# Where an overflow pass stands among 32 streamed experts, and how often their counts are asked

## The chip, the cores and the metric

One core of a Trainium2 chip. The metric is the device time of one execution in microseconds (us); the lower the better. The profiled execution is one such execution with the hardware profiler's records.

## The reference

One block of a streaming encoder on 256 tokens of width 1024: projections, three branches (sparse latent attention, convolution, memory attention), a mix and a layer norm give `h`; then a mixture of experts on `h`, a residual and a last layer norm. What the change touches is the mixture, cut to its core:

```
logits = h @ w_router + b_router                 # 256 x 32
top_v, top_e = top_k(logits, 4)
gate = softmax(top_v)
for e in range(32):                              # tokens that chose e
    g, u = split(h[tokens] @ w1[e] + b1[e], 2)   # w1[e]: 1024 x 2048
    g, u = min(g, 7), clip(u, -7, 7)
    a = (u + 1) * (g * sigmoid(1.702 * g))
    y[tokens] += gate * (a @ w2[e] + b2[e])      # w2[e]: 1024 x 1024
out = layer_norm(alpha * h + y)
```

## The kernel before, in words

Until about 300 us the kernel computes everything up to the router; it counts the tokens of each expert (`cnt`), each token's place within its expert (`pos`) and its gate (`Gt`). Then the experts follow one after another, e0 to e31, and at the end the layer norm.

*Weights.* Each expert has 12 tiles of 1 MB, eight of `w1` and four of `w2`. SP sends them in order (`send`, L107 and L109) into a ring of 20 slots; a send waits until the slot's earlier tile has been used, and what stands behind it on SP waits too. All weights are used once, so that 384 tiles pass through the ring.

*Tokens.* An expert works in blocks of 32 tokens: block 0 always, block 1 only with more than 32 tokens, block 2 with more than 64 (conditionals on the count, which `load` brings into registers of PE, ScalarE and VectorE, L1263). What one expert has beyond 96 goes to passes over a list after e31 (`passes`, `more`), each up to 96 tokens of one expert, which load that expert's 12 tiles again. `more` is nested ten deep; each depth asks the list whether there is another pass (L1296), and an untaken one is left by a branch over all that is nested in it. With this input four experts have three blocks (e5, e8, e10, e25), eight have two (e0, e7, e12, e13, e15, e16, e17, e27), twenty have one; e25 alone has tokens for a pass (44 of them). It can be seen in the trace from the bias products of a block (L1085 into PG, PU, PY), which stand at its start.

*One expert* (`products`, L1175). First products of all blocks into PG, PU and PY (`first`, L1085 for the bias, L1088 for the weights); the scatter of the expert before into the accumulators PO (`scatter`, L1141); the activation on VectorE and ScalarE (`act`, L1092 to L1098); the rows of the next expert, taken out of `h` by a product with a 0/1 matrix (`onehot` L1039, `gather` L1045), which are then transposed (`turn_x`, L1052); the activations transposed (`turn_a`, L1102); second products, in two halves (`second`, L1110 for the bias, L1118), and between them the places of the next expert's tokens (`places`, L1123 and L1124, on PX) and what VectorE makes of them for the scatter (`slots`, L1128, L1129). `split_y` (L1134, L1135) reads the result. A third block shares buffers: its activation waits for that of block 0 (L1190 to L1194), its scatter is done at once (`third_out`, L1161). Conditionals stand after each pair of first products (L1075), around the activation (L1185), the turns (L1190, L1192), the second products (L1075), `split_y` (L1202) and the third blocks (L1233). The engines run the same program; each has its own register and branches by itself.

*e0* has its places and slots made before its products (L1340 to L1344). Its residual (`residual`, L1173) follows its first products.

*The end.* After e31 its scatter, then `more(0, ...)`, then four closing products (L1358), the rows of `r` (L1364) and the layer norm (L1373 to L1387).

The order of the instructions on each engine is that of the code, as a scheduler has slightly shifted it; no table sets it.

Of the kernel before, what the change touches and what calls it, by code (L numbers as in the profile page):

```python
# [75 lines left out]
def tile_block(ctx: ExitStack, tc: tile.TileContext, x, memt, wf, wsm, bp, wdw, rows, w1, b1, w2, b2, out):  # L76
# [995 lines left out]
    def past(n, f, b=1):  # L1072

        if b < 3:
            with tc.If(n > 32 * b):  # L1075
                f(b)
                past(n, f, b + 1)
# [43 lines left out]
    def places(x):  # L1121

        PE.matmul(PX[:, 0:T], lhsT=x.idb.to_broadcast([NE, 128]), rhs=posT, start=True, stop=True)  # L1123
        PE.matmul(PX[:, T:2 * T], lhsT=x.idf.to_broadcast([NE, 128]), rhs=GT, start=True, stop=True)  # L1124

    def slots(x, b, sc, gs):

        V.tensor_scalar(sc, PX[:, 0:T], x.sx[b], None, op0=OP.is_equal)  # L1128
        V.scalar_tensor_tensor(g, sc.bitcast(F32), 1.0, PX[:, T:2 * T], op0=OP.mult,  # L1129
                               op1=OP.mult, accum_out=gs)  # L1130
# [30 lines left out]
    def third_out(x, p):  # L1161

        scatter(s2s[p], y2)
        places(x)
        slots(x, 2, s2s[p], g2[p])
        split_y(PG, g2[p], y2)
# [8 lines left out]
    def products(x, p, n, before=None, rows=None, turned=None, beside=None):  # L1175


        banks = (PG, PU, PY)
        xs = [xcol(xT, 0), xcol(xT, 1), xcol(x2, 0)]
        for k in range(0, KD, 2):  # L1180
            first(x, xs[0], PG, (k, k + 1))
            past(n, lambda b: first(x, xs[b], banks[b], (k, k + 1)))
        before and before()
        act(PG[:, 0:256], PG[:, 256:512], ab[:, 0, :])
        with tc.If(n > 32):  # L1185
            act(PU[:, 0:256], PU[:, 256:512], ab[:, 1, :])
        rows and rows()
        turn_a(ab[:, 0, :], PG[:, 0:256], aT[0])
        turned and turned()
        with tc.If(n > 32):  # L1190
            turn_a(ab[:, 1, :], PU[:, 0:256], aT[1])
            with tc.If(n > 64):  # L1192
                act(PY[:, 0:256], PY[:, 256:512], ab[:, 0, :])
                turn_a(ab[:, 0, :], PG[:, 256:512], aT[2])  # L1194
        outs = (PY, PU, PG)
        second(x, aT[0], PY, 0)
        past(n, lambda b: second(x, aT[b], outs[b], 0))
        beside and beside()
        second(x, aT[0], PY, 1)
        past(n, lambda b: second(x, aT[b], outs[b], 1))  # L1200
        split_y(PY, gc[p], ys)
        with tc.If(n > 32):  # L1202
            split_y(PU, g2[p], y2)
# [4 lines left out]

    def expert(e, prev, n, nxt):
        p = e % 2  # L1210
        x, last = Work(e), nxt is None
        y = None if last else Work(e + 1)

        def before():
            if not e:
                return residual()
            scatter(scs[1 - p], ys)
            with tc.If(prev > 32):
                scatter(s2s[1 - p], y2)

        def beside():
            places(y)
            slots(y, 0, scs[1 - p], gc[1 - p])
            with tc.If(nxt > 32):
                slots(y, 1, s2s[1 - p], g2[1 - p])

        if last:
            products(x, p, n, before)
        else:
            onehot(y, 0, dd)  # L1230
            products(x, p, n, before, lambda: gather(dd), lambda: turn_x(xT), beside)
            send_to(e + 1)
        with tc.If((n if last else n | nxt) > 64):  # L1233
            with tc.If(n > 64):
                third_out(x, p)
            if not last:
                with tc.If(nxt > 64):
                    third_in(y)
# [26 lines left out]

    three_e = [ET.PE, ET.Activation, ET.DVE]

    def count(e):
        return load(cnt[0:1, e:e + 1], three_e, 256) if e < NE else None
# [25 lines left out]
    def more(j, w):  # L1295
        with tc.If(load(ki[0:1, j:j + 1], three_e + [ET.SP], 64) > 0):  # L1296
# [7 lines left out]
            onehot(x, 0, dd)  # L1304
            gather(dd)
            turn_x(xT)
            n = load(un, three_e, 256)
            places(x)
            for b in range(2):
                slots(x, b, (scs, s2s)[b][0], (gc, g2)[b][0])  # L1310
            with tc.If(n > 64):
                third_in(x)
            products(x, 0, n)
            scatter(scs[0], ys)
            with tc.If(n > 32):
                with tc.If(n > 64):
                    third_out(x, 0)
                scatter(s2s[0], y2)
# [12 lines left out]
    tokens_in()  # L1331
# [6 lines left out]
    counts = [None, count(0), None]  # L1338
    x = Work(0)
    places(x)  # L1340
    slots(x, 0, scs[0], gc[0])
    with tc.If(counts[1] > 32):
        slots(x, 1, s2s[0], g2[0])
    with tc.If(counts[1] > 64):  # L1344
        third_in(x)
    for e in range(NE):
        if e == 1:
            passes()
        counts[2] = count(e + 1)
        expert(e, *counts)  # L1350
        counts = counts[1:] + [None]
    scatter(scs[(NE - 1) % 2], ys)
    with tc.If(counts[0] > 32):
        scatter(s2s[(NE - 1) % 2], y2)
    more(0, {b: big("w") for b in [(1, k) for k in range(KD)] + [(2, c) for c in (0, 2, 1, 3)]})
# [103 lines left out]
```

## Time and profile before

| | us |
|---|---|
| median of 3 runs | 1339.78 |
| lowest and highest run | 1336.41, 1343.5 |
| profiled execution | 1340.14 |
| its span, first to last instruction | 1338.4 |
| PE busy (share of the span) | 1096.7 (82%) |
| VectorE busy | 469.5 (35%) |
| ScalarE busy | 291.5 (22%) |
| DMA queue of the kernel, share of 16 engines | 86.1% |

The shares are means over two stages: until 300 us PE works on the branches while little is loaded, afterwards 32 experts are streamed. The windows below cut the second stage. A row of a timeline gives start, duration, engine, line, operation, tiles, the number of instructions drawn together, and in brackets for how long the engine was idle before it and what released it.

### The profile page before, as it was taken

What the parts mean: (1) busy time and instruction counts of PE and PEld (TensorE: products, weight loads), DVE (VectorE), ACT (ScalarE), POOL (GpSimd) and SP (SyncE); (2) the same over time, 40 slices, a digit from 0 to 9 for tenths busy, and PEclk for the clock granted to TensorE, in tenths of its full rate; (3) what the DMA queues carried; (4) which work ended last, traced back from release to release, by engine and by line L of the source; (5) the groups of instructions that cost most, each with busy time, mean ns of one, the idle gap of its engine ahead of it and who ended that gap; (6) DMA issues with size and microseconds to landing.
All of it is one profiled execution on the core that took longest, in us unless ns stands there. A gap on an engine that the chain in (4) does not pass through costs nothing. (4 is left out here: it accounts for less than half of the span.)

```text
span 1338.4 us, 22356 instructions
## 1 busy us (share of the span) xinstructions
PE 1096.7 (82%) x8154; PEld 518.2 (39%) x8154; DVE 469.5 (35%) x1098; ACT 291.5 (22%) x561; POOL 96.3 (7%) x105
## 2 busy tenths in 40 slices
PE   9899889988777888988888888887876698877673
PEld 7788679952222222223222222232221123322121
DVE  6897998762222122221212212222111122221123
ACT  6457875631011010011101101111010001010000
POOL 1406660010000000000000000000000000000001
PEclk9899999999998989989989999999998898999887
DMA  7654258687999999969799999999999999999971
GB/s 272 219 188 132 90 190 318 222 301 315 406 423 419 422 423 422 404 239 404 277 371 417 366 407 423 392 384 420 422 423 421 421 424 422 420 421 421 421 325 66
DMA packets 88075, 464.29 MB, mean 347 GB/s; under 512 B 8209, under 2 KB 8337, under 8 KB 54001
## 3 DMA queue, kind: packets, MB, share of 16 engines
q1 hardware_dynamic: 87888, 461.78, 86.1%
q8 instruction: 120, 1.97, 0.5%
q14 instruction: 67, 0.54, 0.1%
HBM read 460.70 MB, written 1.05 MB: 345 GB/s over the span
## 5 line engine op out<-in xcount | busy, mean ns | idle before, releaser
L1088 PE MATMUL PG<-w,RES 128*32 128x512 f32 x2112 | 293.5, 670 | 40.1 <-PEq L1075 21.7
L1088 PEld LDWEIGHTS PG<-w,RES 128*32 128x32 f32 x2112 | 71.3, 117 | 230.3 <-issue 172.7
L1092 DVE TENSOR_SCALAR RES<-PG 128x256 f32<-128x256 f32 x33 | 14.0, 425 | 402.6 <-PE PG L1088 402.6
L1118 PE MATMUL PY<-w,aa 128*32 128x512 f32 x1056 | 139.7, 622 | 2.0 <-DMA w<-in_w_dram 1.4
L1093 ACT ACTIVATE RES<-RES 128x256 f32<-128x256 f32 x50 | 20.9, 417 | 503.2 <-DVE RES L1092 503.0
L264 PE MATMUL mm<-hh,whi 128*128 128x256 f32 x352 | 102.4, 291 | 6.9 <-DVE gt L799 3.0
L265 PE MATMUL mm<-hl,whi 128*128 128x256 f32 x352 | 99.1, 282 | 4.1 <-DVE hl L364 4.1
L1088 PE MATMUL PU<-w,RES 128*32 128x512 f32 x832 | 100.5, 599 | 0.0
L266 PE MATMUL mm<-hh,wlo 128*128 128x256 f32 x352 | 98.7, 280 | 0.2 <-DVE wlo L218 0.2
L1045 PE MATMUL PX<-h,dd 128*64 128x512 f32 x296 | 77.9, 648 | 24.9 <-DVE dd L1039 13.7
L218 DVE TENSOR_TENSOR wlo<-raw,whi 128x1024 fp32r<-128x1024 f32 (+1 forms) x74 | 92.0, 1252 | 10.1 <-ACT whi L210 6.6
L210 ACT ACTIVATE whi<-raw 128x1024 fp32r<-128x1024 f32 (+1 forms) x74 | 76.0, 1030 | 18.0 <-DMA raw<-in_wf_dram 17.8
L138 POOL TENSOR_TENSOR l20r<-l20a,mhalf 128x1 f32<-128x1 f32 x1 | 0.6, 550 | 1029.5 <-DVE l20a L136 1029.5
L264 PEld LDWEIGHTS mm<-hh,whi 128*128 128x128 f32 x352 | 66.8, 190 | 11.3 <-DVE gt L799 3.2
L1085 PE MATMUL PG<-BB,sel 96*32 96x512 bf16 x128 | 16.1, 460 | 65.5 <-DVEq L1233 50.8
L265 PEld LDWEIGHTS mm<-hl,whi 128*128 128x128 f32 x352 | 66.6, 189 | 4.9 <-DVE hl L364 4.6
L664 POOL TENSOR_TENSOR cv<-cv,ct 128x256 f32<-128x256 f32 x70 | 63.7, 910 | 57.2 <-ACT ct L663 52.6
L266 PEld LDWEIGHTS mm<-hh,wlo 128*128 128x128 f32 x352 | 66.6, 189 | 0.4 <-DVE wlo L218 0.4
L1134 ACT ACTIVATE yy<-PY,gc 128x512 fp32r<-128x512 f32 x33 | 22.7, 687 | 194.2 <-PE PY L1118 187.7
L1128 DVE TENSOR_SCALAR sc<-PX,sx 128x256 fp32r<-128x256 f32 x32 | 15.5, 484 | 133.7 <-PE PX L1124 133.7
L1118 PEld LDWEIGHTS PY<-w,aa 128*32 128x32 f32 x1056 | 40.3, 112 | 52.2 <-issue 35.9
L1118 PE MATMUL PU<-w,aa 128*32 128x512 f32 x416 | 54.9, 599 | 0.0
(363 smaller groups left out, 1386.4 us busy)
## 6 DMA issues: line engine op xcount, KB each, us to landing
w<-in_w_dram SPq DMA_DIRECT2D x396, 1024.0 KB, 18.2
raw<-in_wf_dram SPq DMA_DIRECT2D x70, 512.0 KB, 4.0
rb<-in_rows_dram SPq DMA_DIRECT2D x3, 512.0 KB, 6.1
mT<-in_memt_dram SPq DMA_DIRECT2D x4, 256.0 KB, 5.7
raw<-in_wf_dram SPq DMA_DIRECT2D x4, 256.0 KB, 5.1
xt<-in_x_dram SPq DMA_DIRECT2D x2, 512.0 KB, 6.6
rw<-in_rows_dram SPq DMA_DIRECT2D x2, 512.0 KB, 5.1
r<-in_rows_dram SPq DMA_DIRECT2D x2, 512.0 KB, 4.7
```

Source lines behind the costliest of these rows:

```text
L210: S.activation(parts[i][:, c], raw[i][:, c], AF.Copy)
L218: V.tensor_tensor(lo[:, c], raw[i][:, c], parts[i][:, c].bitcast(F32), op=OP.subtract)
L264: PE.matmul(o, lhsT=wh, rhs=xh, start=first, stop=False)
L265: PE.matmul(o, lhsT=wh, rhs=xl, start=False, stop=False)
L266: PE.matmul(o, lhsT=wl, rhs=xh, start=False, stop=last)
L664: G.tensor_tensor(o, o, ct, op=OP.add)
L1045: PE.matmul(PX[q * 64:q * 64 + 64, :], lhsT=dd[:, t, :].bitcast(F32), rhs=h1[:, t, q * 512:q * 512 + 512], start=t == 0, stop=t == 1)
L1085: PE.matmul(y, lhsT=x.sel.to_broadcast([96, 32]), rhs=BB1[:, :, c], start=True, stop=False)
L1088: PE.matmul(y, lhsT=xs(k), rhs=x.w[1, k][:, :, c], start=False, stop=k == KD - 1)
L1093: S.activation(s, g, AF.Sigmoid, scale=1.702)
L1118: PE.matmul(o[r:r + 32, :], lhsT=aT[:, c:c + 32], rhs=x.w[2, k // 2][:, k % 2, q * 512:q * 512 + 512], start=i == 0 and h > 0, stop=i == 3)
L1134: S.activation(y[0], o, AF.Copy, scale=gs)
```

## The change

It does seven things.

1. The passes (`more`) stand between e30 and e31. The scatter of e30 is done before them, the tiles of e31 are sent behind them, and e31's rows, places and slots are made there; e30 and e31 are no longer interleaved.
2. `count` loads a count into three sets of registers: PE's own (`n[0]`), one of ScalarE and VectorE (`n[1]`), one of all three (`n[2]`). A conditional in which only some engines have work uses their register: the first products PE's, the activation that of the other two.
3. The third block's first products go to PX instead of PY, its activation into a buffer of its own (`aT[3]`), directly behind that of block 1.
4. Turns and first halves of the second products of blocks 1 and 2 stand together in one conditional; second halves, `split_y`, `third_out` and the next expert's `third_in` in another (L1206), on `n | m`, the counts of this expert and the next.
5. The gather stands behind all activations in the code, as before, but now shares PX with the third block's products and activation.
6. The loads of the next count stand behind the scatter instead of at the head of the expert.
7. e0: `tokens_in`, the residual, places and slots stand behind its first products, the places on PY.

```diff
-    def products(x, p, n, before=None, rows=None, turned=None, beside=None):
-        banks = (PG, PU, PY)
+    def products(x, p, n, before=None, y=None, counts=None):
+        banks = (PG, PU, PX)
         xs = [xcol(xT, 0), xcol(xT, 1), xcol(x2, 0)]
         for k in range(0, KD, 2):
             first(x, xs[0], PG, (k, k + 1))
-            past(n, lambda b: first(x, xs[b], banks[b], (k, k + 1)))
+            past(n[0], lambda b: first(x, xs[b], banks[b], (k, k + 1)))
         before and before()
+        m = counts() if y else None
         act(PG[:, 0:256], PG[:, 256:512], ab[:, 0, :])
-        with tc.If(n > 32):
+        with tc.If(n[1] > 32):
             act(PU[:, 0:256], PU[:, 256:512], ab[:, 1, :])
-        rows and rows()
+            with tc.If(n[1] > 64):
+                act(PX[:, 0:256], PX[:, 256:512], aT[3])
+        if y:
+            gather(dd)
         turn_a(ab[:, 0, :], PG[:, 0:256], aT[0])
-        turned and turned()
-        with tc.If(n > 32):
+        if y:
+            turn_x(xT)
+        second(x, aT[0], PY, 0)
+        with tc.If(n[2] > 32):
             turn_a(ab[:, 1, :], PU[:, 0:256], aT[1])
-            with tc.If(n > 64):
-                act(PY[:, 0:256], PY[:, 256:512], ab[:, 0, :])
-                turn_a(ab[:, 0, :], PG[:, 256:512], aT[2])
-        outs = (PY, PU, PG)
-        second(x, aT[0], PY, 0)
-        past(n, lambda b: second(x, aT[b], outs[b], 0))
-        beside and beside()
+            second(x, aT[1], PU, 0)
+            with tc.If(n[2] > 64):
+                turn_a(aT[3], PG[:, 256:512], aT[2])
+                second(x, aT[2], PG, 0)
+        if y:
+            slots_in(y, 1 - p, m, PX)
         second(x, aT[0], PY, 1)
-        past(n, lambda b: second(x, aT[b], outs[b], 1))
         split_y(PY, gc[p], ys)
-        with tc.If(n > 32):
-            split_y(PU, g2[p], y2)
+        with tc.If((n[2] | m[2] if y else n[2]) > 32):
+            with tc.If(n[2] > 32):
+                second(x, aT[1], PU, 1)
+                split_y(PU, g2[p], y2)
+                with tc.If(n[2] > 64):
+                    second(x, aT[2], PG, 1)
+                    third_out(x, p)
+            if y:
+                with tc.If(m[2] > 64):
+                    third_in(y)
+    def flush(p, n):
+        scatter(scs[p], ys)
+        with tc.If(n[0] > 32):
+            scatter(s2s[p], y2)
+    def rows_in(y):
+        onehot(y, 0, dd)
+        gather(dd)
+        turn_x(xT)
+    def slots_in(y, p, m, o):
+        places(y, o)
+        slots(y, o, 0, scs[p], gc[p])
+        with tc.If(m[1] > 32):
+            slots(y, o, 1, s2s[p], g2[p])
     def send_to(e):
         while sent[0] < 12 * e + 12:
             send()
...
+    def loads(a):
+        return [load(a, g, 256) for g in ([ET.PE], [ET.Activation, ET.DVE], three_e)]
     three_e = [ET.PE, ET.Activation, ET.DVE]
     def count(e):
-        return load(cnt[0:1, e:e + 1], three_e, 256) if e < NE else None
+        return loads(cnt[0:1, e:e + 1])
...
             x = More(j, w)
-            onehot(x, 0, dd)
-            gather(dd)
-            turn_x(xT)
-            n = load(un, three_e, 256)
-            places(x)
-            for b in range(2):
-                slots(x, b, (scs, s2s)[b][0], (gc, g2)[b][0])
-            with tc.If(n > 64):
+            rows_in(x)
+            n = loads(un)
+            slots_in(x, 0, n, PX)
+            with tc.If(n[2] > 64):
                 third_in(x)
             products(x, 0, n)
-            scatter(scs[0], ys)
-            with tc.If(n > 32):
-                with tc.If(n > 64):
-                    third_out(x, 0)
-                scatter(s2s[0], y2)
+            flush(0, n)
             if j + 1 < NX:
                 more(j + 1, w)
...
     turn_x(xT, True)
-    tokens_in()
...
-    counts = [None, count(0), None]
-    x = Work(0)
-    places(x)
-    slots(x, 0, scs[0], gc[0])
-    with tc.If(counts[1] > 32):
-        slots(x, 1, s2s[0], g2[0])
-    with tc.If(counts[1] > 64):
-        third_in(x)
+    n, m = count(0), None
+    with tc.If(n[2] > 64):
+        third_in(Work(0))
+    prev = None
     for e in range(NE):
         if e == 1:
             passes()
-        counts[2] = count(e + 1)
-        expert(e, *counts)
-        counts = counts[1:] + [None]
-    scatter(scs[(NE - 1) % 2], ys)
-    with tc.If(counts[0] > 32):
-        scatter(s2s[(NE - 1) % 2], y2)
-    more(0, {b: big("w") for b in [(1, k) for k in range(KD)] + [(2, c) for c in (0, 2, 1, 3)]})
+        p = e % 2
+        x, y = Work(e), Work(e + 1) if e < NE - 2 else None
+        def before():
+            nonlocal m
+            if not e:
+                tokens_in()
+                residual()
+                slots_in(x, 0, n, PY)
+            elif e < NE - 1:
+                flush(1 - p, prev)
+            if y:
+                m = count(e + 1)
+        if y:
+            onehot(y, 0, dd)
+        products(x, p, n, before, y, lambda: m)
+        if y:
+            send_to(e + 1)
+            prev, n = n, m
+        elif e == NE - 2:
+            flush(p, n)
+            more(0, {b: big("w") for b in [(1, k) for k in range(KD)] + [(2, c) for c in (0, 2, 1, 3)]})
+            send_to(e + 1)
+            n = count(e + 1)
+            rows_in(Work(e + 1))
+            slots_in(Work(e + 1), 1 - p, n, PX)
+            with tc.If(n[2] > 64):
+                third_in(Work(e + 1))
+    flush(p, n)
```

(`n[2] | m[2]` is a bitwise or.) Two places of the programs as built, in the order in which an engine meets the rows.

SP, from the last tiles of the innermost pass on, before (`w` is a weight tile, `r` the rows of the last layer norm; PE_49 and the like are the counters on which a row waits):

```order
L1302 DMA w<-in_w_dram 128x2x1024 [waits DMAHW6_49,PE_49]
L1075 UNCONDITIONAL_BRANCH
L1202 UNCONDITIONAL_BRANCH
L1315 UNCONDITIONAL_BRANCH
L1296 UNCONDITIONAL_BRANCH [waits SP_sequencer_49,DMAHW0_49,DMAHW1_49,DMAHW2_49,DMAHW3_49,DMAHW4_49,DMAHW5_49,DMAHW6_49,DMAHW7_49] x10
L1364 DMA r_16752<-in_rows_dram 128x1024 [waits DMAHW7_49,PE_49,Activation_49]
```

and now (L1297 and L1303 are the old L1296 and L1302):

```order
L1303 DMA w<-in_w_dram 128x2x1024 [waits DMAHW2_49,PE_49]
L1206 UNCONDITIONAL_BRANCH
L1219 UNCONDITIONAL_BRANCH
L1297 UNCONDITIONAL_BRANCH [waits SP_sequencer_49,DMAHW0_49,DMAHW1_49,DMAHW2_49,DMAHW3_49,DMAHW4_49,DMAHW5_49,DMAHW6_49,DMAHW7_49] x10
L107 DMA w<-in_w_dram 128x2048 [waits DMAHW7_49,DMAHW3_49,PE_49]
L107 DMA w<-in_w_dram 128x2048 [waits DMAHW4_49,DMAHW2_49,DMAHW6_49,DMAHW1_49,PE_49]
L107 DMA w<-in_w_dram 128x2048 [waits DMAHW5_49,DMAHW1_49]
```

The tiles of e31 (L107) were sent ahead of the passes and now stand behind the branch over them; the first two wait on a count of PE that is reached in the last use of a pass's tile in the program, in the tenth nested pass.

PE, from the end of e0's first products (the third block's) to the gather of e1's rows, before:

```order
L1088 MATMUL PY<-w,RES 32x512 [waits Activation_49]
L1088 MATMUL PY<-w,RES 32x512 x7
L1075 UNCONDITIONAL_BRANCH
L1075 UNCONDITIONAL_BRANCH [waits PE_49] x2
L1173 MATMUL PO_3503<-h_3399,ab 128x512 [waits DVE_49,Pool_49]
...
L1185 COMPARE_AND_BRANCH
L1185 UNCONDITIONAL_BRANCH x2
L1045 MATMUL PX<-h_3399,dd 64x512 [waits Activation_49]
```

and now:

```order
L1088 MATMUL PX<-w,RES 32x512 [waits DVE_49,Activation_49]
L1088 MATMUL PX<-w,RES 32x512 x7
L1075 UNCONDITIONAL_BRANCH
L1075 UNCONDITIONAL_BRANCH [waits PE_49] x2
L1023 MATMUL PY<-ident,pos 32x128 x2
L1173 MATMUL PO_3503<-h_3399,ab 128x512 [waits DVE_49,Pool_49]
...
L1123 MATMUL PY<-posT,idb 128x256
L1124 MATMUL PY<-tl,ident 128x256
L1260 TENSOR_LOAD cnt x2
L1045 MATMUL PX<-h_3399,dd 64x512 [waits DVE_49,Activation_49]
```

Between the first products and the gather stand the transposes of `pos` and `Gt` (L1023), the places (L1123, L1124) and the loads of e1's count; the gather waits on VectorE too, and PE has no conditional around the activation any more.

## Rows read from the trace of the kernel before

**Rows 1.** Windows of the second stage; the last columns: granted clock, DMA share, GB/s.

```profile
350.00:550.00 200.00, 162.90 (x1212) 54.74 (x1212) 42.67 (x125) 22.01 (x47) 0.00 (x0) 0.93 1.02 422
550.00:610.00 60.00, 52.52 (x412) 18.84 (x408) 13.03 (x37) 6.59 (x15) 0.00 (x0) 0.94 0.79 309
...
890.00:1290.00 400.00, 308.85 (x2177) 101.41 (x2181) 76.66 (x231) 37.99 (x81) 0.00 (x0) 0.92 1.02 420
```

**Rows 2.** PE timeline of e19 (one block), with its start and the next.

```profile
913.45 0.43 PE L1085 MATMUL PG<-BB,sel 96*32 96x512 bf16 x4 [2.37 <-DVEq L1233]
...
925.34 1.94 PE L1045 MATMUL PX<-h,dd 128*64 128x512 f32 x8 [0.57 <-DVE ab L1098]
...
929.33 0.39 PE L1110 MATMUL PY<-BB,sel 96*32 96x512 bf16 x2 [0.64 <-DVEq L1190]
...
936.55 0.43 PE L1085 MATMUL PG<-BB,sel 96*32 96x512 bf16 x4 [2.37 <-DVEq L1233]
```

**Rows 3.** VectorE timeline of e19: activation from L1092 to L1098, slots L1128.

```profile
923.46 0.42 DVE L1092 TENSOR_SCALAR RES<-PG 128x256 f32<-128x256 f32 x1 [9.42 <-PE PG L1088]
...
924.90 0.49 DVE L1098 SCALAR_TENSOR_TENSOR ab<-ab,RES 128x128 f32<-128x128 f32 x2
...
932.36 0.48 DVE L1128 TENSOR_SCALAR sc<-PX,sx 128x256 fp32r<-128x256 f32 x1 [3.14 <-PE PX L1124]
```

**Rows 4.** PE timeline of e8 (three blocks), start, middle and the next start.

```profile
545.47 0.41 PE L1085 MATMUL PG<-BB,sel 96*32 96x512 bf16 x4
...
574.75 0.44 PE L1102 MATMUL PG<-ident,ab 128*128 128x128 f32 x2 [2.28 <-DVE ab L1098]
...
575.29 2.91 PE L1118 MATMUL PY<-w,aa 128*32 128x512 f32 x16
...
593.50 0.65 PE L1085 MATMUL PG<-BB,sel 96*32 96x512 bf16 x4 [3.01 <-DVEq L1237]
```

**Rows 5.** VectorE timeline of e8: the third block's activation starts.

```profile
572.89 0.41 DVE L1092 TENSOR_SCALAR RES<-PY 128x256 f32<-128x256 f32 x1
```

**Rows 6.** PE timeline of e0: first products, residual, gather, and e1's start.

```profile
300.48 3.19 PE L1088 MATMUL PG<-w,RES 128*32 128x512 f32 x16
...
318.58 3.67 PE L1173 MATMUL PO<-h,ab 128*128 128x512 f32 x8 [0.56 <-DVE ab L1098]
...
322.18 1.94 PE L1045 MATMUL PX<-h,dd 128*64 128x512 f32 x8
...
337.15 0.43 PE L1085 MATMUL PG<-BB,sel 96*32 96x512 bf16 x4 [1.98 <-DVE lg L1251]
```

**Rows 7.** PE timeline: last products of e30, of e31, scatters, closing products.

```profile
1243.68 1.92 PE L1118 MATMUL PY<-w,aa 128*32 128x512 f32 x16
...
1272.27 1.91 PE L1118 MATMUL PY<-w,aa 128*32 128x512 f32 x12 [1.39 <-DMA w<-in_w_dram]
...
1275.82 0.96 PE L1141 MATMUL PO<-yy,sc 64*128 64x512 f32 x6 [0.23 <-DVEq L1202]
...
1318.92 1.20 PE L1141 MATMUL PO<-y__3521,s 64*128 64x512 f32 x8 [0.31 <-PEq L1316]
1324.07 0.27 PE L1358 MATMUL PO<-one,tri 128*128 128x1 bf16 x4 [3.95 <-PEq L1296]
```

**Rows 8.** On PE: the branches at L1233, and the count loads; ns minimum/median/maximum.

```profile
L1233 PEldq COMPARE_BRANCH  x32: 67/215/440, 336.2 to 1274.7; - x32
...
L1263 PEldq TENSOR_LOAD <-cnt x32: 297/306/487, 298.2 to 1224.3; - x32
```

**Rows 9.** PE's branches at L1296, SP's wait for them, the rows of r.

```profile
L1296 PEldq COMPARE_BRANCH  x3: 70/179/3892, 1277.4 to 1323.8; - x3
...
SPq L1364 <- PEq L1296: 21.4, 1, 21.4
...
1323.67 2.03 SPq L1364 DMA_DIRECT2D r<-in_rows_dram  x2
...
DMA to landing us min/median/max: 3.8/4.7/5.6
```

More of the change, by code (lines that the diff above doesn't have):

```diff
@@ L1119, in second, with places, slots @@
                               start=i == 0 and h > 0, stop=i == 3)
[L1121 to L1129, printed above, removed]
+    def places(x, o):
+        PE.matmul(o[:, 0:T], lhsT=x.idb.to_broadcast([NE, 128]), rhs=posT, start=True, stop=True)
+        PE.matmul(o[:, T:2 * T], lhsT=x.idf.to_broadcast([NE, 128]), rhs=GT, start=True, stop=True)
+    def slots(x, o, b, sc, gs):
+        V.tensor_scalar(sc, o[:, 0:T], x.sx[b], None, op0=OP.is_equal)
+        V.scalar_tensor_tensor(g, sc.bitcast(F32), 1.0, o[:, T:2 * T], op0=OP.mult,
                                op1=OP.mult, accum_out=gs)
@@ L1163, in third_out @@
         scatter(s2s[p], y2)
-        places(x)
-        slots(x, 2, s2s[p], g2[p])
+        places(x, PX)
+        slots(x, PX, 2, s2s[p], g2[p])
         split_y(PG, g2[p], y2)
@@ L1207, in send_to @@
             send()
[L1209 to L1233, printed above, removed]
-            with tc.If(n > 64):
[L1235 to L1238, printed above, removed]
     NX = 10
@@ L1303, in more @@
             x = More(j, w)
-            onehot(x, 0, dd)
-            gather(dd)
-            turn_x(xT)
-            n = load(un, three_e, 256)
-            places(x)
-            for b in range(2):
-                slots(x, b, (scs, s2s)[b][0], (gc, g2)[b][0])
-            with tc.If(n > 64):
+            rows_in(x)
+            n = loads(un)
+            slots_in(x, 0, n, PX)
+            with tc.If(n[2] > 64):
                 third_in(x)
             products(x, 0, n)
-            scatter(scs[0], ys)
-            with tc.If(n > 32):
-                with tc.If(n > 64):
-                    third_out(x, 0)
-                scatter(s2s[0], y2)
+            flush(0, n)
             if j + 1 < NX:
@@ L1337, in tile_block @@
     send_to(0)
-    counts = [None, count(0), None]
-    x = Work(0)
-    places(x)
-    slots(x, 0, scs[0], gc[0])
-    with tc.If(counts[1] > 32):
-        slots(x, 1, s2s[0], g2[0])
-    with tc.If(counts[1] > 64):
-        third_in(x)
+    n, m = count(0), None
+    with tc.If(n[2] > 64):
+        third_in(Work(0))
+    prev = None
     for e in range(NE):
```

## The prediction

> **What bounds the kernel now.** I read the windows first, then PE's, VectorE's and SP's timelines, then the waits. From 350 to 550 us and again from 890 to 1290 the DMA share is 1.02 and the stream moves 420 to 422 GB/s; between 550 and 610 it falls to 0.79 and 309 GB/s [rows 1]. An expert is 12 tiles of 1.049 MB, so at 420 GB/s a tile takes 2.5 us and an expert 30. A one-block ("light") expert takes PE 23.1 us from one first bias product to the next (e19, 913.45 to 936.55 [rows 2]), a three-block ("hot") one 48.0 (e8, 545.47 to 593.50 [rows 4]); a two-block ("mid") one lies between. So the ring of 20 slots (50 us of stream) fills in the hot and mid experts, and when it is full SP cannot send: the reader sees it in the window of e8, from 550 on. The DMA's idle time up to 890 is set by **PE**. After 890 the **stream** sets the time: nothing that PE saves there counts. What PE saves from e0 to e17 moves the whole stream earlier (call it G); what comes after the stream's last tile counts in full. These two are the sum.
>
> **G, part by part.** *Light experts.* In e19 PE waits 0.57 at the gather, 0.64 at L1110 and 2.37 at L1085 [rows 2]. L1110 waits for VectorE's walk over the conditional L1190, which is gone: -0.64. The wait at L1085 holds PE's last products (to 934.17), split_y, two conditionals (L1202, L1233) and a register load; one conditional and the load leave: -0.4 (estimate). Against it, the gather now also waits, through PX, for both engines' walk over the new conditional behind the activation: +0.44 taken (an estimate), between 0 (it waits for the activation today, 0.57) and 1.0 (its 1.94 us no longer cover what ends later). Hence about -0.77 with the branch behind `second` that is gone too (0.17); six such experts before e18 give -4.6, and two ahead of a hot one, -0.5 each, -5.6 in all.
> *Hot experts* (e5, e8, e10). In e8 the third block's activation starts at 572.89 [rows 5], because it waits for block 0's buffer, and PE stands 2.28 us at 574.75; the next 16 products take 2.91 us [rows 4] where 16 take 1.92 elsewhere [rows 7]. The activation now goes to a buffer of its own directly behind the second, some 5 us sooner, under the scatter of e7. Then the gather, two transposes and block 0's products follow: these start near 572.7 instead of 575.3. Two new stalls appear, since blocks 1 and 2 are now turned right before their products: each waits about 0.8 for its copies. With -2.5 from the start, -2.2 from products that no longer run slowly, +1.6 from the stalls, a last step unchanged (3.01 before L1085 either way), I take -3.0, bounds -1 and -5: three times, **-9.1**.
> *Loads.* Two more register loads per expert on PE, 0.31 each [rows 8], stand where PE waits for the activation anyway: 0, or 0.6 if that wait should go.
> *Mid experts.* The second block is turned late there too (+0.9), the wait at L1110 (0.6) and part of the end leave (-0.3 to -0.4): 0 each, +0.2 in all.
> *e0.* Its products start earlier: PX's places no longer stand before them, 297.3 for 300.48, so they end near 314.8 instead of 318.0 (the residual's start less its wait [rows 6]). But then come, one behind the other: four transposes (0.9, as two of L1102 [rows 4]) and VectorE's two copies (0.8, as two of L1092 [rows 3]), residual 3.67 [rows 6], places (0.8), slots for two blocks on VectorE (2.0: L1128 at 0.48 [rows 3] and its partner, twice), two register loads (0.6 [rows 8]), and only then two activations of 1.93 each (L1092's start to L1098's end [rows 3]). Before, both ran under the residual, and the gather began at 322.18 [rows 6]. Now 314.8 + 12.6 = 327.4, **+5.2**; the 12 tiles of e0 come free that much later, and the sends that wait for them. PE has idled some 7 us there, and I add 1.4 for slower products behind that (the 16 that took 2.91 or 3.19 instead of 1.92 followed such gaps [rows 4, 6]). Bounds: +0.5, if slots and loads hide, and +8.
> *Clock.* The granted clock is 0.92 to 0.94 in these windows [rows 1]; slow stretches like e8's follow gaps of PE, of which some shrink: 0 to -5, taken -1.7.
> So G = 5.6 + 9.1 - 0.2 - 6.6 + 1.7 = **9.6**, with ends of 1 and 18.
>
> **The end.** Today: e30's last products end at 1245.60, e31's at 1274.18, 1.91 behind its last tile, its scatter at 1276.78, and the pass follows; its scatter ends at 1320.12 [rows 7]. PE then walks over nine nested passes: one branch of 3.892 us; SP has waited 21.4 us for that before it sends the rows of `r` at 1323.67 [rows 9], and L1358 runs at 1324.07 [rows 7]. With the pass ahead of e31, all of this moves up by e31's 28.58 us: pass end 1291.5, branch and signal to 1295.1. **e31's twelve tiles stand behind it.** The order of SP shows their sends behind the branch over the nested passes, and the first two wait on PE's counter as `r`'s send does today: the slots are those of the pass's tiles, whose last use in the program stands in the last nested pass. So nothing of e31 is loaded while the pass computes. From 1295.1 I count 1.9 until the stream runs (half of the 3.8 that the quicker of `r`'s two loads took to land [rows 9]; ends 1 and 3.8), 12 x 2.5 = 30.0, then 1.9 to the last product and 2.6 to the end of the scatter as today: 1331.5. The preparation of e31 (gather, places) lies under the load, and so do its first products. From L1358 to the span's end today are 14.3 us, of which VectorE waits 0.7 for `r`, which now comes earlier: 13.6, with 0.4 to reach it. 1345.5 against 1338.4: **+7.1**, ends +5.5 and +9.5. The pass itself is costed at no change: its tiles take the place in the stream that e31's had, and they land before its products ask for them.
>
> [...] PE's branch over the nested passes takes 3.892 us, that over L1233's 30 rows 0.215 in the median and 0.44 at most [rows 8]. The new L1206 jumps over 36 rows on PE; I cost it as L1233's. [...]
>
> **Sum.** 1340.1 + 7.1 - 9.6 = 1337.6 against the profiled run (1340.14, 0.4 above the median of the three runs, which themselves lie 7 us apart); against the median **1337.2**. Change by over 0.5%, about what a measurement of this kernel can tell from none, begins at 1333.1 and 1346.5.
>
> **Rivals.**
> 1. *PE gains more* (0.17): the hot experts gain 5 each and no stretch behind a shorter gap is slow: G = 16 to 18, about 1329.5. For it: e8's slow products stand right behind its 2.28 us wait [rows 4]. Against: the new 0.8 us stalls and e0's long idle.
> 2. *The move hides the load* (0.05): e31's tiles stream under the pass. Then pass end 1291.5, branch 3.6, preparation 6.5, products 18, and 16.6 of scatter and end: 1336.2, less G: 1327. SP's order and the 21.4 us wait of `r` [rows 9] speak against it.
> 3. *A far skip* (0.05): L1206's skip costs 3.9. It is walked between two light experts; three such pairs lie before e18, each 3.9 less the 2 us that split_y takes anyway: +6, 1343.
> 4. *Slower: the gather behind the activations* (0.13). The gather now stands behind every activation of an expert, and turn_a behind the gather. With the upper bound of 1.0 instead of 0.4 in each of eight light experts, 1.0 more in each of six mid ones and e0 at +8, G falls by 4.8 + 6 + 1.4 to -2.6: 1349. It is slower than 1346.5 from G < 0.3. Against: the gather waits for VectorE's activation in e19 already [rows 2].
> My forecast has 0.60, with 1333 to 1345 as its own range. **Range** 1328 to 1346.5, which leaves out the outer halves of 1, 2 and 4. Faster 0.27 (rivals 1 and 2, and the forecast's lower edge 0.05), slower 0.12 (rival 4 without its edge, and a little of the forecast), same 0.61.
>
> **What would show it.** Right: DMA idle for some 20 us right before e31's first product, PE's last product 1.9 us behind the last tile; e1 starting 5 to 7 us later than 337.15 [rows 6]; no wait over 1 us at L1102 of the third block; no L1110 wait in light experts. Wrong: tiles of e31 landing before the pass's scatter ends, a stream that is not earlier at e18, or a light expert's L1085 wait above 2.4 us.

## The result: 1.2% faster, below the forecast range

| | us |
|---|---|
| the changed kernel, median of 4 runs (lowest, highest) | 1323.69 (1322.43, 1328.53) |
| before, 4 runs in all | 1341.64 (1336.41, 1343.92) |
| ratio, 95% interval | 0.9878 [0.9838, 0.9919] |
| again, both on one chip (a_plain, 6 runs; before, 11) | 1323.12 and 1339.04, 0.9877 [0.9847, 0.9907] |
| forecast and range | 1337.2 (1328 to 1346.5) |

The forecast said no measurable change; the kernel is faster by 16 to 18 us, 4 us below the range. The tail came as costed. G, the gain of PE up to e18, did not: e18 starts 21.2 us earlier in this profile and 17.0 in a second one of the same program (a_plain), where 9.6 stood.

The windows of the changed kernel, to be read beside [rows 1]:

```profile
350.00:550.00 200.00, 166.21 (x1324) 55.16 (x1320) 44.37 (x130) 22.67 (x48) 0.00 (x0) 0.99 1.02 422
550.00:610.00 60.00, 51.10 (x392) 17.88 (x385) 16.13 (x46) 8.10 (x17) 0.00 (x0) 0.97 1.01 414
...
890.00:1290.00 400.00, 304.89 (x2170) 92.75 (x2174) 74.79 (x224) 37.24 (x79) 0.00 (x0) 0.92 0.95 394
```

Two columns differ: between 550 and 610 us the stream no longer pauses (DMA share 1.01 for 0.79), and the granted clock, third from the right, is 0.97 to 0.99 instead of 0.93 to 0.94. The last window now holds the pause in front of e31's tiles.

The whole way from e1's start to e18's, as one window, before (337.15 to 890.84):

```profile
337.15:890.84 553.69, 460.46 (x3548) 158.65 (x3548) 121.86 (x361) 58.72 (x127) 0.00 (x0) 0.95 0.95 388
```

in the changed kernel, and in a second profile of the same program (a_plain):

```profile
344.76:869.69 524.93, 442.05 (x3549) 147.44 (x3549) 122.95 (x362) 59.75 (x127) 0.00 (x0) 0.99 0.99 409
```

```profile
343.01:873.83 530.82, 449.70 (x3549) 148.84 (x3549) 122.87 (x362) 59.71 (x127) 0.00 (x0) 0.97 0.98 405
```

PE does the same 3548 products (one record more or less). It is idle for 93.2 us before (553.69 - 460.46) and 82.9 and 81.1 now: 10 to 12 us. The products themselves took 460.5 us and now take 442.1 and 449.7: 11 to 18 us, at a mean clock of 0.99 and 0.97 instead of 0.95. So of the 28.8 and 22.9 us by which this stretch is shorter, 18.4 and 10.8 are not waiting that went, but the same products in less time, at that higher mean clock, and the two profiles of one program differ in how much of it they got.

One-block expert e19, PE, beside [rows 2]:

```profile
890.10 0.40 PE L1085 MATMUL PG<-BB,sel 96*32 96x512 bf16 x4 [1.65 <-DVEq L1206]
890.33 1.89 PE L1088 MATMUL PG<-w,RES 128*32 128x512 f32 x16
...
901.51 1.94 PE L1045 MATMUL PX<-h,dd 128*64 128x512 f32 x8 [1.11 <-DVEq L1186]
...
904.77 0.39 PE L1110 MATMUL PY<-BB,sel 96*32 96x512 bf16 x2
...
911.28 0.40 PE L1085 MATMUL PG<-BB,sel 96*32 96x512 bf16 x4 [1.65 <-DVEq L1206]
```

21.2 us for 23.1. The wait at L1110 is gone, the gather's is 1.11 for 0.57, and the gap at L1085 is 1.65 for 2.37. The 16 products behind that gap take 1.89 us. Before, they took 3.36, as this row of the kernel before shows:

```profile
913.67 3.36 PE L1088 MATMUL PG<-w,RES 128*32 128x512 f32 x16
```

The windows from the same place on, before and in the changed kernel (granted clock third from the right):

```profile
913.40:916.80 3.40, 3.35 (x20) 0.86 (x19) 0.42 (x2) 0.00 (x0) 0.00 (x0) 0.59 1.00 419
```

```profile
890.10:893.50 3.40, 3.21 (x32) 0.97 (x36) 0.42 (x2) 0.00 (x0) 0.00 (x0) 1.00 1.01 419
```

In the window with a clock of 0.59 the 16 products took 3.36 us, in the one with 1.00 they took 1.89.

Three-block expert e8, PE, beside [rows 4]:

```profile
568.65 0.39 PE L1110 MATMUL PU<-BB,sel 96*32 96x512 bf16 x2 [0.69 <-ACT aa L1104]
...
571.89 0.39 PE L1110 MATMUL PG<-BB,sel 96*32 96x512 bf16 x2 [0.76 <-ACT aa L1104]
...
584.33 0.40 PE L1085 MATMUL PG<-BB,sel 96*32 96x512 bf16 x4 [2.63 <-DVEq L1214]
584.55 2.92 PE L1088 MATMUL PG<-w,RES 128*32 128x512 f32 x16
```

The two new stalls are there, 0.69 and 0.76 (0.8 each was taken). The gap behind a three-block expert is still 2.63, and slow products still follow it (2.92 us for 16, 1.89 in e19).

e0, PE, beside [rows 6]:

```profile
317.17 3.67 PE L1173 MATMUL PO<-h,ab 128*128 128x512 f32 x8 [1.06 <-DVE ab L1170]
...
327.94 3.68 PE L1045 MATMUL PX<-h,dd 128*64 128x512 f32 x8 [6.45 <-DVEq L1188]
...
344.76 0.40 PE L1085 MATMUL PG<-BB,sel 96*32 96x512 bf16 x4 [1.65 <-DVEq L1210]
```

The gather began at 327.94 (327.4 was worked out), after 6.45 us of idle time, and ran slowly (3.68 us for 1.94 [rows 6]). That the two agree so closely is luck in this profile: the stage ahead ended 4.5 us later than before, and e0's first 16 products took 1.90 us and not 3.19. In a_plain, which has neither, the gather begins at 326.35.

The end, PE's timeline, beside [rows 7]:

```profile
1219.68 3.20 PE L1118 MATMUL PY<-w,aa 128*32 128x512 f32 x12 [1.41 <-DMA w<-in_w_dram]
...
1266.08 1.20 PE L1141 MATMUL PO<-y__3521,s 64*128 64x512 f32 x8
1271.91 3.33 PE L1045 MATMUL PX<-h,dd 128*64 128x512 f32 x8 [4.63 <-PEq L1260]
...
1304.16 1.91 PE L1118 MATMUL PY<-w,aa 128*32 128x512 f32 x12 [0.42 <-DMA w<-in_w_dram]
...
1308.83 0.24 PE L1370 MATMUL PO<-one,tri 128*128 128x1 bf16 x4 [0.15 <-PEq L1219]
```

and what SP waited for there, its timeline, and PE's branches at L1297 (ns, minimum, median, maximum):

```profile
SPq L107 <- PEq L1297: 19.9, 1, 19.9
```

```profile
1270.53 5.15 SPq L107 DMA_DIRECT2D w<-in_w_dram  x8
```

```profile
L1297 PEldq COMPARE_BRANCH  x3: 70/179/3647, 1226.2 to 1270.8; - x3
```

The pass ends at 1267.28, PE leaves the nested passes by a branch of 3.647 us, and only then, 19.9 us late, does SP send e31's first tile. From e30's last product (1222.88) to the span's end are 99.3 us; before they were 92.8 (1338.4 - 1245.60 [rows 7]). So the tail costs +6.5, and e30's last product is 22.7 us earlier. In a_plain the same way is 99.4 us long.

### The profile page after: what moved, and what is told of

Same layout as the page of the kernel before. It is cut to its first block, busy times and chain, and to the rows that moved or that the text cites. A ratio compares the mean times of both kernels' runs of the same rounds, so it can differ in the third digit from the quotient of the medians.

```text
span 1322.2 us, 21503 instructions
## 1 busy us (share of the span) xinstructions
PE 1084.3 (82%) x8154; PEld 503.6 (38%) x8154; DVE 471.0 (36%) x1098; ACT 292.9 (22%) x561; POOL 96.5 (7%) x105
## 5 line engine op out<-in xcount | busy, mean ns | idle before, releaser
L1088 PE MATMUL PG<-w,RES 128*32 128x512 f32 x2112 | 280.5, 643 | 52.9 <-DMA w<-in_w_dram 29.1
L1088 PEld LDWEIGHTS PG<-w,RES 128*32 128x32 f32 x2112 | 62.6, 113 | 241.8 <-issue 153.4
L1092 DVE TENSOR_SCALAR RES<-PG 128x256 f32<-128x256 f32 x33 | 14.0, 425 | 387.8 <-PE PG L1088 387.2
L1088 PE MATMUL PU<-w,RES 128*32 128x512 f32 x832 | 98.7, 592 | 0.0
L218 DVE TENSOR_TENSOR wlo<-raw,whi 128x1024 fp32r<-128x1024 f32 (+1 forms) x74 | 92.1, 1252 | 11.4 <-ACT whi L210 6.0
L1134 ACT ACTIVATE yy<-PY,gc 128x512 fp32r<-128x512 f32 x33 | 22.7, 687 | 152.4 <-PE PY L1118 136.7
L1085 PE MATMUL PG<-BB,sel 96*32 96x512 bf16 x128 | 13.0, 396 | 48.3 <-DVEq L1206 14.9
L1047 ACT ACTIVATE RES<-PX 128x512 f32<-128x512 f32 x37 | 22.1, 597 | 137.1 <-PE PX L1045 137.1
L1118 PE MATMUL PU<-w,aa 128*32 128x512 f32 x416 | 51.9, 593 | 0.0
```

Source lines behind the costliest of these rows:

```text
L218: V.tensor_tensor(lo[:, c], raw[i][:, c], parts[i][:, c].bitcast(F32), op=OP.subtract)
L1047: S.activation(xr, PX, AF.Copy)
L1088: PE.matmul(y, lhsT=xs(k), rhs=x.w[1, k][:, :, c], start=False, stop=k == KD - 1)
L1118: PE.matmul(o[r:r + 32, :], lhsT=aT[:, c:c + 32], rhs=x.w[2, k // 2][:, k % 2, q * 512:q * 512 + 512], start=i == 0 and h > 0, stop=i == 3)
L1134: S.activation(y[0], o, AF.Copy, scale=gs)
```

## The experiments

Theory **C** (clock): the part of the gain that the forecast missed are products that no longer run at a lower granted clock (0.59 in the window of e19 before, 1.00 now), since the gaps of PE ahead of them have become short (2.37 and 1.65 us there). Rival **I** (idle time): shorter waits alone. Rival **M**: the move of the passes is the gain. Open beside them: what e0's new order costs, and what the three registers bring. Each ratio is to before as measured on the same chip. The chips differ from run to run, so that a difference to 1323.69 is a rough one; the ratio of the changed kernel, 0.9878 [0.9838, 0.9919] and 0.9877 [0.9847, 0.9907], is what a variant's ratio is to be held against.

**a_heads: only the loads of the count put back** (changed kernel).

```diff
         def before():
-            nonlocal m
...
                 flush(1 - p, prev)
-            if y:
-                m = count(e + 1)
...
         if y:
+            m = count(e + 1)
             onehot(y, 0, dd)
```

> The changed kernel with the loads of the next count put back at the head of each expert, in front of its first products: 0.6 us more on PE behind a gap of 1.65 us, so that the gap of a one-block expert is 2.2 to 2.4 us again, as before the change. Theory C: slow products come back behind these gaps; from e1 to e18 PE's busy time, 442 us in the changed kernel for the same instructions, rises by 6 to 15 us on top of 4 to 10 us of idle time, and the time grows by 8 to 20 us. Theory I: busy time stays at 442 within 2; only idle time comes, 4 to 10 us.

1342.67 (12 runs) against 1338.46 for before: 1.0037 [1.0016, 1.0058]. The loads go from behind the scatter back to the head of the expert. Two register loads of 0.3 us on PE per expert, moved within the expert, cost 19 us (21 by the ratios) and turn the whole change into a loss. The same stretch, e1 to e18, and the start of e3 with its clock:

```profile
344.81:889.01 544.20, 455.36 (x3549) 159.50 (x3548) 123.24 (x362) 59.79 (x127) 0.00 (x0) 0.97 0.97 395
```

```profile
388.93 0.43 PE L1085 MATMUL PG<-BB,sel 96*32 96x512 bf16 x4 [2.42 <-DVEq L1206]
389.14 3.11 PE L1088 MATMUL PG<-w,RES 128*32 128x512 f32 x16
```

```profile
388.90:392.30 3.40, 3.32 (x20) 0.74 (x19) 0.42 (x2) 0.00 (x0) 0.00 (x0) 0.63 1.03 425
```

The gap is 2.42 again, the products behind it take 3.11 us at a clock of 0.63. Idle time is 88.8 us, 6 to 8 more than in the changed kernel; busy time 455.4, 6 to 13 more. This stretch is 13 to 19 us longer, of which 6 to 8 are idle time: C's expectation came, and rival I, which expected busy time to stay at 442, falls here.

**b_loads: only the loads moved** (kernel before).

```diff
-        counts[2] = count(e + 1)
-        expert(e, *counts)
...
+                scatter(scs[1 - p], ys)
...
+            nxt = count(e + 1)
```

> The kernel before with one part of the change alone: the load of the next count stands behind the scatter instead of at the head of the expert. It takes 0.3 us out of the gap in front of L1085 (2.37 to about 2.06 in one-block experts, 1.97 to 1.66 in two-block ones). Theory C (gaps of 2.3 us and more are followed by products at the lower clock, gaps of 1.65 are not): besides 5 us of idle time up to e18 some of the slow products go, 2 to 8 us of PE's busy time; 5 to 13 us faster. Theory I (idle time alone): 5 us or less, busy time from e1 to e18 unchanged at 460 within 2.

The load goes from the head of the expert to behind the scatter. 1336.04 (12 runs) against 1339.49, 0.9963 [0.9942, 0.9984]: 3.5 us faster by the medians (2 to 8 by the interval).

```profile
336.45:885.31 548.86, 456.73 (x3548) 151.44 (x3548) 121.80 (x362) 58.79 (x127) 0.00 (x0) 0.96 0.96 392
```

Busy time 456.7 for 460.5, idle 92.1 for 93.2. The gaps were mostly 2.04 to 2.06 behind one-block experts (2.37 before, 1.65 in the changed kernel), and four of the eight of these up to 1000 us were still followed by slow products. Less than half of the step in the gap brought a part of the gain, by busy time (-3.7) rather than idle time (-1.1). The time is at or below the lower end of what C expected (5 to 13) and within what rival I expected (5 or less); the busy time fell as C says and is not unchanged within 2, as rival I says.

**b_fill: the gaps filled, nothing else** (kernel before).

```diff
         past(n, lambda b: second(x, aT[b], outs[b], 1))
+        warm(PX, 8)
```

> The kernel before, with one addition: behind each expert's last second products PE does eight more products (bias rows times ones, into PX) that nobody reads, in the gap of 2.0 to 2.4 us in which it waited for the end of the expert. Nothing is taken off the chain of waits. Theory C (clock): the gain that the forecast missed came from products that ran at the lower granted clock behind such gaps and no longer do. Then the filled gaps alone raise the granted clock between 350 and 550 us from 0.93 to 0.97 or more, the first products' mean falls from 653 ns towards 615, and the time falls by 6 to 13 us. Theory I (idle time): the gain came from shorter waits alone. Then the clock's records may move, but the time stays within 3 us of before, or grows where the added products delay the next start.

1337.16 (12 runs) against 1338.46, 0.9974 [0.9953, 0.9995].

```profile
338.44:884.98 546.54, 475.25 (x3684) 173.58 (x3684) 121.41 (x358) 58.70 (x127) 0.00 (x0) 0.98 0.96 393
```

```profile
L955 PE MATMUL PX<-BB,one 96*128 96x512 bf16 x136 | 32.2, 379 | 4.2 <-PEq L1075 4.2
```

The clock's part is as C says: the granted clock from 350 to 550 us is 0.99 for 0.93, and without the 136 added products (32.2 us) PE's busy time is 443.1 for 460.5, 17 us less, by nothing but work that nobody reads. But the rest of the stretch, idle or filled, grew from 93.2 to 103.5, since the filling delays what comes behind it; the way from e1 to e18 is 7.1 us shorter in this profile, and the median gained 1.3 us. As a time, C's 6 to 13 us were missed, and what rival I expected (within 3 us of before) came. What this run shows is that filling the gaps alone raised the clock, and with it the products' busy time fell; that such busy time also comes off the time of a run, it doesn't show, since the filling takes back what the products give.

**a_hotfill: the last gaps of over 2 us filled** (changed kernel, passes and e0 as in a_both below).

```diff
                     third_out(x, p)
+                    warm(PX, 6)
```

> The changed kernel with the passes behind e31, e0's old order, and six products that nobody reads behind the third block of an expert, in the last gaps of over 2 us (2.63 before the expert that follows a three-block one). Theory C: the first products of the expert behind it no longer run slowly, 1.4 us for each of three experts before e18, 3 to 5 us faster than the same kernel without them (1314.8), so near 1311, and PE's gap there falls to about 1.3. Theory I: no gain, within 2 us of 1314.8.

1317.1 (6 runs), 0.9839 [0.9806, 0.9872], against 0.9813 [0.9781, 0.9846] without the filling: no gain. Behind e8 and e10 the first 16 products took 1.89 us, behind e5 (the row of the next start shows 0.42 us of wait) 3.34:

```profile
471.42 1.46 PE L955 MATMUL PX<-BB,one 96*128 96x512 bf16 x6 [1.04 <-DVE RES L1129]
473.29 0.62 PE L1085 MATMUL PG<-BB,sel 96*32 96x512 bf16 x4 [0.42 <-DVEq L1215]
```

and the added products took PE's time. C's expectation failed here; rival I expected no gain.

**b_pass and a_pass_last: the pass moved alone, and moved back alone.** Kernel before with its `more(0, ...)` between e30 and e31, e31 prepared behind it; changed kernel with it at the end:

```diff
-        x, y = Work(e), Work(e + 1) if e < NE - 2 else None
+        x, y = Work(e), Work(e + 1) if e < NE - 1 else None
...
-        elif e == NE - 2:
...
     flush(p, n)
+    more(0, {b: big("w") for b in [(1, k) for k in range(KD)] + [(2, c) for c in (0, 2, 1, 3)]})
```

> The kernel before with one part of the change alone: the pass stands between e30 and e31, and e31's rows and places are made behind it. Both theories C and I, and the forecast: e31's tiles are sent only when PE has left the nested passes, about 20 us in which nothing is loaded, so 5.5 to 9.5 us slower (about 7) than before. Rival M (the move itself is what makes the changed kernel faster): 5 us or more faster than before.

> The changed kernel with the passes back behind e31, which is interleaved with e30 again. Theories C and I, and the forecast's second term: 5.5 to 9.5 us faster than the changed kernel (about 6.6, the distance from e30's last product to the end being 99.3 us in the changed kernel and 92.8 in the one before), so near 1317. Rival M: slower than the changed kernel.

The edit shown is a_pass_last's. b_pass 1346.08 (12 runs) against 1338.46, 1.0042 [1.0020, 1.0064]: 5.6 us slower by the ratio, clear of noise. a_pass_last 1316.2 (6 runs), 0.9835 [0.9801, 0.9869], 7.5 us under the changed kernel's 1323.69 (5.8 by the ratios, whose intervals overlap). M falls by b_pass alone, and a_pass_last agrees: the move of the passes costs some 6 us.

**a_e0_back, a_plain, a_e0_again, a_both: e0's old order**, in the changed kernel (twice, the second time beside the unchanged a_plain on one chip) and together with the passes at the end.

```diff
     turn_x(xT, True)
+    tokens_in()
...
     n, m = count(0), None
+    slots_in(Work(0), 0, n, PX)
...
-                tokens_in()
                 residual()
-                slots_in(x, 0, n, PY)
```

> The changed kernel with e0's order put back: its tokens, places and slots are made before its first products, the residual alone behind them. The forecast's term: e1 starts 5 to 8 us earlier than at 344.76, and since the ring is full later on (DMA share 0.80 between 640 and 680 us in the changed kernel) the whole stream moves by as much: 5 to 8 us faster than the changed kernel, near 1317. Rival: the stream's idle time behind e1 is used up elsewhere, and the end moves by less than 3 us.

> The changed kernel with e0's old order, once more beside the changed kernel on one chip. In the traces e1 starts 5 to 6 us earlier with the old order. Theory S (the whole stream moves with e1): 4 to 6 us faster than the changed kernel. Theory N (what e0 loses is made up before the stream limits): within 2 us of it.

> The changed kernel with the passes behind e31 again and e0's old order. If the two terms add (7.5 measured for the passes, 5 to 8 expected for e0): 12 to 15 us faster than the changed kernel, near 1310. If the DMA's remaining idle time (about 15 us between 610 and 890 us in the changed kernel) limits the sum: 8 to 11.

a_e0_back 1324.87 (6 runs), a_e0_again 1322.75 against a_plain's 1323.12 (6 runs each; 0.9863 [0.9828, 0.9898] and 0.9877 [0.9847, 0.9907]), a_both 1314.78 (6 runs) against a_pass_last's 1316.2: +1, 0, -1. a_both lies in its lower range (8 to 11 us under the changed kernel), but nearly all of that is the passes'. The 5 to 8 us of e0 were not there; what remains is under what these runs can tell. One half of the reason is in the traces: e0's own way isn't 6 us longer. The last products ahead of the experts (L1000, the counts) stand here in two profiles of the changed program (the first result, then a_plain), and in a_e0_again and a_both:

```profile
290.99 0.20 PE L1000 MATMUL PG<-Mb,one 128*128 128x32 bf16 x2
```

```profile
286.09 0.20 PE L1000 MATMUL PG<-Mb,one 128*128 128x32 bf16 x2
```

```profile
289.45 0.20 PE L1000 MATMUL PG<-Mb,one 128*128 128x32 bf16 x2
```

```profile
286.06 0.20 PE L1000 MATMUL PG<-Mb,one 128*128 128x32 bf16 x2
```

The stage ahead of e0 ends at 286 to 287 or at 289 to 291, run by run, also for one and the same program. From there to e1's start are 53.8 and 56.9 us with the new order (344.76 and 343.01), 52.3 and 52.2 with the old (341.70 and 338.25), 50.6 in the kernel before. So the new order costs 2 to 5 us of e0 and not 5 to 8. Why not even those show in the medians was not settled.

**a_one_reg: one register for all three engines** (changed kernel).

```diff
-        return [load(a, g, 256) for g in ([ET.PE], [ET.Activation, ET.DVE], three_e)]
+        return [load(a, three_e, 256)] * 3
```

> The changed kernel with one count register for all three engines instead of three sets: VectorE and ScalarE again walk the conditionals between the first products, PE that around the activation. They have 15 us of idle time there, and PE loses one load of 0.31 us where it waits for the activation anyway. Theory C: PE's gap in front of L1085 stays at 1.65, so nothing comes back: within 3 us of the changed kernel. Rival R (the separate registers carry the gain): 5 us or more slower.

1329.21 (6 runs), 0.9914 [0.9882, 0.9946]: 5.5 us above 1323.69, which is on R's side, but the intervals of the two ratios overlap. The gaps at L1085 were those of the changed kernel (1.65, three of 2.63 and one of 2.21), and the way from e1 to e18 takes 530.6 us, as in a_plain (530.8). Between C and R this run doesn't decide.

**The gaps, counted.** Over the eleven profiles without added products (before, the changed kernel twice, and eight runs of variants), from 340 to 1000 us, counted from the records: the gaps of over 1.5 us in front of L1085, and how many of them were followed within 6 us by at least four first products of over 0.9 us each (the median of the products of L1088 is 0.59, before and in the changed kernel):

| gap, us | number | followed by slow products |
|---|---|---|
| 1.6 to 1.8 | 115 | 1 |
| 1.8 to 2.2 | 21 | 6 |
| 2.2 to 2.5 | 37 | 19 |
| 2.5 to 2.85 | 30 | 26 |
| 2.85 and more | 10 | 9 |

A slow start costs 1.2 to 1.5 us in the two rows above (3.11 and 3.36 against 1.89). Of before's 18 gaps 12 lie in the second and third line and six below; of the changed kernel's 20, 16 lie in the first line, and the three of 2.63 behind three-block experts in the fourth. A gap's length goes with the kind of expert in front of it, so that the table alone doesn't separate the two; a_heads and b_fill, which leave the experts as they are, do.

**Clock and time, run by run.** Whether the clock comes off the time as well can be read from the runs of one and the same program, since each has its own mean granted clock. The 29 runs of the kernel before that were measured beside b_fill have clocks of 0.934 to 0.949 and times of 1333.49 to 1346.25 us; a straight line through them falls by 0.76 us for each 0.001 of clock (correlation -0.82). The 17 runs beside b_loads and the 11 beside a_plain give 0.83 and 0.80 (-0.86 and -0.64). From 0.9395, the mean of these 11, to a_plain's 0.953 this line gives 11 us: an estimate of the clock's share of the 16 us there. A correlation doesn't say which of the two moves the other; it agrees with C, and it is not a proof.

## Why the prediction was wrong, step by step

- **What bounds the kernel**: right. G showed up as an earlier stream (DMA share 1.01 for 0.79 from 550 to 610), and e18 starts 21.2 us earlier. From there to e30's last product the stream takes as long as before, 353.2 us for 354.8.
- **The end, +7.1**: right in mechanism and size: +6.5 in the profile, +5.6 by b_pass, +5.8 to +7.5 by a_pass_last. The 3.9 us branch (3.647), SP's wait (19.9) and the 12 tiles behind it (from 1270.53 to the last product's wait at 1304.16: 33.6, against 31.9 worked out) came as written.
- **e0, +6.6**: e1 started 7.6 us later, but 4.5 of these came from a stage ahead of it that varies. Counted from L1000 it is 3.2, and 6.3 in a_plain. Undoing it brought no time that could be measured.
- **Hot experts, -9.1** (three times 3.0 is 9.0): -7.9 by their starts in the two traces (e5 49.2 to 45.8, e8 48.0 to 45.5, e10 47.9 to 45.9), -5.1 in a_plain. Right in mechanism and within its bounds, with the 2.2 us of slow products that was counted there; the closeness of the first figure is in part luck.
- **Light experts, -5.6 in all, mid experts, +0.2, and *Loads*, 0**: here it failed. By their starts the eight light experts before e18 gained 16.2 us (14.4 in a_plain) and the six mid ones 4.7 (3.4). The waits themselves came out near: in e19 the one at L1110 left (-0.64 as written), the gather's grew by 0.54 (0.44 taken), the gap at L1085 shrank by 0.72 (0.4 taken). But behind that gap another 1.5 us of slow products went, and e19 gained 1.9. The forecast counted the load that leaves the gap at its own length, within the 0.4, and its new place at nothing; what hangs on the gap besides its length, it did not count. a_heads, which puts the loads back, costs 19 us.
- **Clock, -1.7, ends 0 to -5**: the term that was mis-sized, and the step that failed. Beside the 6.6 us in the hot experts, slow products were taken as a side effect; in all 8.3 us of busy time were forecast to go, and 11 to 18 went. The rows to see it in were at hand: a mean clock of 0.93 over 200 us in [rows 1] costs up to 14 us in that window alone (0.07 x 200), an estimate that takes the products' time to go as the clock does (in the two windows of e19 above 1.89 us is 0.56 of 3.36, and the clocks are 0.59 and 1.00), and the slow products stand behind the same L1085 gap that the light experts' term shortened. G's upper end of 18 us held 5 us for the clock; with 18 the time is 1328.9, and so the range's 1328 was too high.
- **Idle time** from e1 to e18: 7.9 forecast (16.2 less the 8.3), 10 to 12 measured.
- **The signs**: those of being right came (SP sends e31's tiles 19.9 us late, no wait over 1 us at L1102 of e8's third block, no L1110 wait in e19; e1 5.9 us later in a_plain, 7.6 in the first profile), and none of those of being wrong. They test the tail, e0 and the waits; none was set on the clock, and so none could show the term that failed.
- **Rival 1** (PE gains more, 0.17) comes nearest in time (1329.5), but not by its mechanism: the hot experts gained 2.0 to 3.4 us each, not 5, and e8's gap of 2.63 is still followed by slow products. The gain came by the light experts. **Rival 2** fell: no tile of e31 lands under the pass. **Rival 3** fell as a cost: L1206's branch on PE has a median of 0.078 us, but two of its 33 took 2.9 us, one of them between the light experts e1 and e2:

```profile
L1206 PEldq COMPARE_BRANCH  x33: 76/78/2959, 339.6 to 1304.2; - x33
L1206 PEldq COMPARE_BRANCH  x1: 2909/2909/2909, 361.7 to 361.7; - x1
```

  The gap in front of e2 is 1.68 us all the same, and it ends with VectorE, so that this branch cost nothing. What makes these two and the 3.647 at L1297 so long, no run here shows.

- **Rival 4** fell: the gather's wait grew to 1.11 in e19, less than what left elsewhere.

a_both has the lowest median: 1314.78, 0.9813 [0.9781, 0.9846] of before, where a_plain has 0.9877 [0.9847, 0.9907]. It keeps the new body of an expert, and puts the passes and e0 back.

## What to carry to other kernels

Where PE works in short stretches, look at the gaps ahead of its products and at how long the first products behind each take; a register load that is cheap by itself (0.3 us) lengthens a gap, and with the gap grew here the share of starts with slow products (1 of 115 behind 1.6 to 1.8 us, 19 of 37 behind 2.2 to 2.5). In a_heads 0.6 us in each of 17 experts, 10 us in all, made the way from e1 to e18 13 to 19 us longer. A part of a program that is skipped by a branch still ordered the transfers behind it here, since they use its slots (19.9 us on SP). Undo each part of a bundle alone: here one part costs some 6 us, and another, counted at 0.4 us of a gap, decides the sign.

## What was not expected of the hardware

Whether products ran slowly behind a gap could be told from its length only at the ends: 1 of 115 did at 1.6 to 1.8 us and 9 of 10 at 2.85 us and more, but 19 of 37 at 2.2 to 2.5 us. One program's profiles differ by it: the two of the changed kernel have 442.1 and 449.7 us of busy time for the same products.

The same shows ahead of the experts. That stage ended between 286.06 and 290.99 us, though the change doesn't touch it. In the four profiles where it ended latest (the changed kernel's first, a_heads, a_e0_back, a_e0_again) the granted clock between 190 and 210 us was 0.83, in the nine others 1.00. From 199 to 207 us, behind a gap of 2.99 us in the changed kernel's first profile and one of 2.98 in a_plain:

```profile
199.00:207.00 8.00, 6.41 (x32) 6.41 (x33) 6.90 (x12) 1.58 (x3) 0.00 (x0) 0.57 1.00 396
```

```profile
199.00:207.00 8.00, 8.00 (x71) 8.00 (x70) 7.72 (x13) 2.62 (x4) 0.00 (x0) 1.00 1.01 409
```

Behind two gaps of the same length the clock of the window was 0.57 in one and 1.00 in the other. This is a part of the 4.9 us between the two profiles: 2.4 of them stand already in front of that gap (200.59 and 198.19), and why was not settled.
